# Softmax attention logits as three half-array products per head in two banks, in a written order

## The chip, the cores and the metric

The kernel runs on one core of one Trainium2 chip. A core has a matrix engine (TensorE, PE in the profile; its weight loads are listed apart, as PEld), a vector engine (VectorE, DVE), a scalar engine (ScalarE, ACT), a general one (GpSimd, POOL) and an engine that issues transfers (SyncE, SP). Each works through its own queue in order; semaphores tie the queues together. Matrix products are written to banks of PSUM, of 512 floats for each of 128 partitions, and read from there by DVE and ACT. The metric is the device time of one execution in microseconds (us). Before the change it is 2425.18 us, the median of 3 runs (2423.69 to 2426.76).

## What is computed

One decoder layer for 256 positions of width 2048 in float32: a SwiGLU network, a pair of token mixers beside each other (retention with 8 heads, and attention in a sliding window with 32 query heads over 8 key heads of dimension 64), and a second SwiGLU network. All projections of the mixers come from one product `h @ w_in`. The change is in the window attention:

```
def swa_with_sinks(q, k, v, sinks):
    ...
    kb, vb = band(k), band(v)
    logits = jnp.einsum('bnqhgd,bnkhd->bnhgqk', qb, kb).astype(jnp.float32) * (d ** -0.5)
    ...
    logits = jnp.where(valid[None, :, None, None], logits, NEG_INF)
    ...
    probs = jax.nn.softmax(jnp.concatenate([logits, sink], axis=-1), axis=-1)[..., :-1]
    out = jnp.einsum('bnhgqk,bnkhd->bnqhgd', probs.astype(v.dtype), vb)
```

The 256 positions are two blocks of 128. A query sees the 128 keys that end with its own position, or fewer at the start.

## The kernel before

**The large products.** Everything is done as products of 128x128 weights against 512 columns. A weight matrix is loaded as float32 (`raw`), cast to a short form by ACT (`wh`, L356), and the remainder is made by DVE (`wl`, L357). The activations are split in the same way (`hh`, `hl`). One product is then three matmuls, hi by hi, lo by hi and hi by lo (L348 to L350), which gather in two banks `pa`, one for each block `t` of 128 positions. One pass over 512 columns of a weight matrix is called a chunk here; its result needs two of the four banks of the pool `psa`. So the first product of a chunk can only start when the readers of the chunk before the last are done with their bank. Tiles called `raw`, `wh`, `wl` and `pa` come from pools, and a new one waits until the old one in its place has been read for the last time.

**The order of the chunks.** For `w_in` the chunks come as the queries of the window heads (four chunks), and later those of retention: its queries (RQ0, RQ1), its keys (RK0, RK1) and its values (RV0 and on). Retention's queries and keys are turned by a rotary embedding, which DVE does straight from the bank: L1326 (by the cosine) and L1332 (by the sine, twice), and L1337 and L1338 on what they gave. L227 is the sum on DVE that makes the layer's conditioning, of weights that stream in for it.

**The side work.** Between the matmuls of the chunks, generators in the list `side` run one step for each quarter of the depth of a chunk. For the window attention each pair of heads (16 pairs) is one generator, `window(pair)`. In its first step `window_weights` makes the logits, masks and exponentials; in the next one the weights of the pair before are turned by four transposes (L1253), masked (L1262, L1263), multiplied with the values (`window_values`, L1267 and L1275, of 64 columns, the two heads on the two column halves of the array) and copied out by ACT (L1278). Their banks `pd` come from the pool `psd` of two, taken by `side_bank()`.

**The logits.** Head dimension 64 takes half of the 128 partitions. The queries of each head are kept with the hi part on one half of the partitions and the lo part on the other; the keys (`keys`, `homes`, `other`) are there on both halves. A matmul over 128 partitions so adds hi and lo of the query at once, and two of them, with hi and lo of the key, make a logit: four products, lo by lo among them. For a pair there are four matmuls with 256 columns (block 1: both halves of its window) in one bank and four with 128 columns (block 0) in the other (L1201). DVE reads them by L1208 (times the masks), L1209 (add) and L1210 (scale and mask of block 0), L1216 takes the maximum.

**What sets the order.** A scheduler decides the order of the instructions on each engine, by a model of costs; nothing in the window's code is ordered by hand. Each engine then keeps that order.

**The query split.** For a chunk of queries and a block, four transposes (L1301) put the queries into a bank; then, for each of two halves, ACT casts (L1307) and DVE subtracts on 64 partitions.

Of the kernel before, what the change touches and what calls it, by code (L numbers as in the profile page):

```python
# [9 lines left out]
F32 = mybir.dt.float32  # L10
F32R = mybir.dt.float32r
AF = mybir.ActivationFunctionType
ALU = mybir.AluOpType
# [3 lines left out]
P = 128  # L17
S = 256
# [12 lines left out]
QH, KVH, HD = 32, 8, 64  # L31
# [46 lines left out]
def layer_kernel(  # L78
# [22 lines left out]
    nc = tc.nc  # L101
# [16 lines left out]
    def nm(s):  # L118
        uid[0] += 1
        return f"{s}_{uid[0]}"  # L120
# [4 lines left out]
    def bank():  # L125
        return psm.tile([P, CH], F32, tag="ps", name=nm("ps"))

    def side_bank():
        return psd.tile([P, CH], F32, tag="pd", name=nm("pd"))

    def t512():
        return tmp.tile([P, CH], F32, tag="t512", name=nm("t"))
# [7 lines left out]
    def small(n, tag):  # L140
        return two.tile([P, n], F32, tag=tag, name=nm(tag))
# [218 lines left out]
    def pair_tile():  # L360
        return asp.tile([P, 2, CH], F32, tag="a", name=nm("a"))
# [46 lines left out]
    def gemm(act, w, col0s, KT=KD, ready=None):  # L408
        banks = [[acc_bank() for _ in range(NT)] for _ in col0s]
        for kb in range(KT // KB):  # L410
            gemm_part(act, w, col0s, banks, kb, KT, ready if kb == 0 else None)
            step()
        return banks
# [454 lines left out]
    banks, moved = {}, set()  # L868
# [104 lines left out]
    with tc.manual_schedule(engines=ORDERED):  # L973
# [21 lines left out]
        for _ in range(3):  # L995
# [8 lines left out]
            out=s2, in_=ssq.rearrange("p (t i) -> p t i", t=NT), axis=AX.X, op=ALU.add  # L1004
        )
        nc.vector.tensor_scalar(
            out=v2, in0=s2, scalar1=1.0 / D, scalar2=EPS, op0=ALU.mult, op1=ALU.add
# [6 lines left out]
            out=q2, in0=q2, scalar1=-0.5, scalar2=1.5, op0=ALU.mult, op1=ALU.add  # L1014
# [85 lines left out]
    for g, ks in enumerate(groups):  # L1100
# [7 lines left out]
        for i, n in enumerate(order):  # L1108
            if i < first_i:
                continue  # L1110
            at = i - first_i
# [25 lines left out]
    def in_chunk(c0, ready=None):  # L1137
        return gemm(held, wi, [c0], ready=ready)[0]
# [10 lines left out]
    keys = one.tile([P, 2, KVH, S], F32R, tag="x", name="keys")  # L1149
    b = in_chunk(O_SV, ready)  # L1150
    for t in range(NT):
        for g in range(2):
# [8 lines left out]
            for j in range(4):  # L1161
                js = slice(j * P, (j + 1) * P)
                nc.tensor.transpose(ps[:, js], kd[:, js], ident)
            hi, lo = (
                keys[:, i, g * 4 : g * 4 + 4, t * P : (t + 1) * P] for i in range(2)
            )
            p4 = ps.rearrange("p (h s) -> p h s", h=4)
# [4 lines left out]
    for t in range(NT):  # L1172
# [4 lines left out]
    queries = [  # L1177
        v.rearrange("p (j a s) -> p j a s", j=4, a=2)
        for v in (homes[:, : KD * P], other, homes[:, : KD * P], homes[:, KD * P :])
    ]  # L1180
# [3 lines left out]
    pick, causal, own = masks[:, : 2 * P], masks[:, 2 * P : 3 * P], masks[:, 3 * P :]  # L1184

    def twice(v):
        return v[:, None, :].broadcast_to([P, 2, v.shape[1]])

    def window_weights(pair):


        kv = pair // 2
        both = pair_tile()
        lg, parts = both[:, :, :S], both[:, :, S:]
        banks = [side_bank(), side_bank()[:, :S]]
        of_t = [v.rearrange("p (i s) -> p i s", i=2) for v in banks][::-1]
        for i in range(2):
            qs = queries[pair // 4][:, pair % 4, i, :]
            for t in (1, 0):
                for n in range(2):  # L1200
                    nc.tensor.matmul(  # L1201
                        of_t[t][:, i, :],
                        qs[:, t * P : (t + 1) * P],
                        keys[:, n, kv, : (t + 1) * P],
                        start=n == 0,
                        stop=n == 1,
                    )
        nc.vector.tensor_mul(parts, of_t[1], twice(pick))  # L1208
        nc.vector.tensor_add(lg[:, :, :P], parts[:, :, :P], parts[:, :, P:])  # L1209
        nc.vector.scalar_tensor_tensor(  # L1210
            out=lg[:, :, P:], in0=of_t[0], scalar=HD**-0.5, in1=twice(causal),
            op0=ALU.mult, op1=ALU.add,
        )
        mx = small(4, "mx")
        m2 = mx.rearrange("p (i t) -> p i t", t=2)
        nc.vector.tensor_reduce(  # L1216
            out=m2, in_=lg.rearrange("p i (t s) -> p i t s", t=2), axis=AX.X, op=ALU.max
        )
        sb = sink_b[:, 2 * pair : 2 * pair + 2]
        nc.vector.tensor_tensor(  # L1220
            out=m2, in0=m2, in1=sb[:, :, None].broadcast_to([P, 2, 2]), op=ALU.max
        )
        ng = small(4, "ng")
        nc.vector.tensor_scalar(out=ng, in0=mx, scalar1=-1.0, scalar2=None, op0=ALU.mult)
        se = small(4, "se")
        nc.vector.tensor_tensor(
            out=se.rearrange("p (i t) -> p i t", t=2),
            in0=ng.rearrange("p (i t) -> p i t", t=2),
            in1=sb[:, :, None].broadcast_to([P, 2, 2]),
            op=ALU.add,  # L1230
        )
        nc.scalar.activation(se, se, AF.Exp)
        sm = small(4, "sm")
        for i in range(2):
            for z in (2 * i, 2 * i + 1):
                seg = lg[:, i, z % 2 * P : (z % 2 + 1) * P]
                nc.scalar.activation(
                    seg, seg, AF.Exp, bias=ng[:, z : z + 1], accum_out=sm[:, z : z + 1]
                )
        nc.vector.tensor_add(sm, sm, se)  # L1240
        nc.vector.reciprocal(sm, sm)
        l4 = lg.rearrange("p i (t s) -> p i t s", t=2)
        s4 = sm.rearrange("p (i t) -> p i t", t=2)[:, :, :, None]
        nc.vector.tensor_mul(l4, l4, s4.broadcast_to([P, 2, 2, P]))
        return lg
# [36 lines left out]
    def window(pair):  # L1282
        lg = window_weights(pair)
        yield
        if before:
            window_values(*before.pop())
        before.append((pair, lg))
        if pair == QH // 2 - 1:
            yield
            window_values(*before.pop())  # L1290
        yield

    for ci in range(4):
        b = in_chunk(O_SQ + ci * CH)
        for t in range(NT):
            u = t512()
            nc.any.tensor_copy(u, b[t])
            ps = bank()
            for j in range(4):
                js = slice(j * P, (j + 1) * P)  # L1300
                nc.tensor.transpose(ps[:, js], u[:, js], ident)  # L1301
            q4 = queries[ci]
            p4 = ps.rearrange("p (j s) -> p j s", j=4)
            for a in range(2):
                here, there = (slice(c * HD, (c + 1) * HD) for c in (a, 1 - a))
                hi = q4[here, :, a, t * P : (t + 1) * P]
                nc.scalar.copy(hi, p4[here])  # L1307
                nc.vector.tensor_sub(
                    q4[there, :, a, t * P : (t + 1) * P], p4[here], hi.bitcast(F32)
                )  # L1310
        side += [window(pair) for pair in range(ci * 4, ci * 4 + 4)]


# [1 line left out]
    for a, off in ((0, O_RQ), (1, O_RK)):  # L1315
        for ci in range(2):
            b = in_chunk(off + ci * CH)
            for t in range(NT):
                u = t512()
                v = t512()  # L1320
                p4 = b[t].rearrange("p (h a d) -> p h a d", h=4, a=2)
# [107 lines left out]
    for p in range(2):  # L1429
        sg = first if p == 0 else gates(p)  # L1430
        c0s = [(2 * p + i) * CH for i in range(2)]
        for g, a, w in ((1, a_swa, w_swa_branch), (0, a_ret, w_ret_branch)):
            banks = gemm(a, w[0], c0s)
# [109 lines left out]
```

## Time and profile before

The profiled execution took 2424.6 us; its span, from the first instruction's start to the last one's end, is 2422.8 us, so 1.8 us lie around it.

| what | value |
|---|---|
| median of 3 runs | 2425.18 us |
| profiled execution: time, span | 2424.6 us, 2422.8 us |
| mean granted TensorE clock | 0.995 |
| window attention's logits (L1201): first and last start | 853.3, 1082.9 us |
| logits matmuls (L1201) in the trace | 128, half of 256 columns and half of 128 |
| subtraction of weights (L357, DVE) | 784 times, 1205 ns each |
| cast of weights (L356, ACT) | 784 times, 1040 ns each |

In rows of a timeline the columns are the start in us, the duration in us, the engine, the line, the operation, the tiles written and read, and the shape; behind a time in square brackets stands the idle time before it and what ended it. Rows with "x4" stand for four instructions in a row, and their duration reaches from the first start to the last end. A matmul's duration is longer than its share of the stream, since matmuls overlap: the distance from start to start tells what one costs. In rows of lines, the columns are the engine, the line, the operation, the tiles, the count, the duration in nanoseconds (least, median, most), and the first and last start.

### The profile page before, as it was taken

How to read it: one execution, taken by the hardware profiler on the slowest of the kernel's cores; microseconds unless marked ns; L12 is line 12 of the kernel's file. 1: busy time of each engine (PE TensorE's matmuls, PEld its weight loads, DVE VectorE, ACT ScalarE, POOL GpSimd, SP SyncE). 2: the span in 40 equal slices, each digit the busy share in tenths (PEclk: the TensorE clock that was granted, in tenths of full speed). 3: DMA queues.
4: the chain of work that ended last, by engine and by line, in shares of the span. 5: the costliest groups of instructions: out<-in, count | busy, mean ns of one | idle time of the engine just before them, and what ended most of it. 6: DMA issues, size and time to landing. Idle time of an engine off the chain costs nothing.

```text
span 2422.8 us, 28701 instructions
## 1 busy us (share of the span) xinstructions
PE 2389.5 (99%) x10820; PEld 1965.7 (81%) x10820; DVE 1710.0 (71%) x2497; ACT 1184.8 (49%) x1604; POOL 8.3 (0%) x19
## 2 busy tenths in 40 slices
PE   7999999999999999999999999999999999999998
PEld 5887888888888888778888888888888888888886
DVE  7888787778977688886666776768565555545656
ACT  6644554444446455554444444456444444444544
POOL 0000000000000000000000000000000000000000
PEclk9999999999999999999999999999999999999999
DMA  9987668988876666656677777755666666665563
GB/s 362 336 293 287 224 259 330 341 314 322 319 280 230 231 238 213 239 207 227 243 261 255 249 260 274 265 191 191 211 242 224 226 226 234 235 224 190 185 200 122
DMA packets 244542, 603.32 MB, mean 249 GB/s; under 512 B 9809, under 2 KB 10193, under 8 KB 224817
## 3 DMA queue, kind: packets, MB, share of 16 engines
q1 hardware_dynamic: 242850, 591.61, 68.6%
q0 software_dynamic: 1552, 9.87, 1.1%
q8 instruction: 85, 1.39, 0.2%
q14 instruction: 55, 0.45, 0.1%
HBM read 597.22 MB, written 4.22 MB: 248 GB/s over the span
## 4 chain that ended last, share of the span: by engine, by line
PE 95%; DMA 2%; DVE 2%; issue 0%; ACT 0%; SPq 0%; DVEq 0%; ACTq 0%
PE pa L350 29%; PE pa L349 29%; PE pa L348 28%; PE pa L724 1%; DMA slot<-in_w_ada_dram 1%; PE pd L348 1%; PE pd L350 1%; PE pd L349 1%; PE ps L466 1%; PE pd L1201 1%; DVE wl L357 0%; PE pd L1267 0%; DMA x_sb<-in_x_dram 0%; PE pd L1253 0%; DVE slot L227 0%
## 5 line engine op out<-in xcount | busy, mean ns | idle before, releaser
L357 DVE TENSOR_TENSOR wl<-raw,wh 128x1024 fp32r<-128x1024 f32 (+1 forms) x784 | 941.0, 1205 | 586.5 <-ACT wh L356 584.8
L356 ACT CAST wh<-raw 128x1024 fp32r<-128x1024 f32 (+1 forms) x784 | 815.2, 1040 | 997.2 <-PE pa L349 941.7
L348 PE MATMUL pa<-wh,hh 128*128 128x512 f32 x2014 | 788.2, 391 | 3.9 <-DVE t L1332 3.0
L349 PE MATMUL pa<-wh,hl 128*128 128x512 f32 x2014 | 787.0, 391 | 0.0
L350 PE MATMUL pa<-wl,hh 128*128 128x512 f32 x2014 | 725.9, 392 | 0.0
L348 PEld LDWEIGHTS pa<-wh,hh 128*128 128x128 f32 x2014 | 378.7, 188 | 82.9 <-ACT wh L356 5.1
L349 PEld LDWEIGHTS pa<-wh,hl 128*128 128x128 f32 x2014 | 378.7, 188 | 77.1
L350 PEld LDWEIGHTS pa<-wl,hh 128*128 128x128 f32 x2014 | 376.6, 188 | 76.4
L349 PE MATMUL pa<-wh,a 128*128 128x512 f32 x992 | 384.1, 389 | 0.7 <-DVE a L389 0.7
L348 PE MATMUL pa<-wh,a 128*128 128x512 f32 x992 | 367.2, 390 | 1.1 <-ACT wh L356 0.9
L350 PE MATMUL pa<-wl,a 128*128 128x512 f32 x992 | 367.0, 390 | 0.6 <-DVE wl L357 0.6
L348 PEld LDWEIGHTS pa<-wh,a 128*128 128x128 f32 x992 | 185.8, 188 | 41.3 <-ACT wh L356 1.8
L349 PEld LDWEIGHTS pa<-wh,a 128*128 128x128 f32 x992 | 186.2, 188 | 40.0 <-DVE a L389 1.5
L350 PEld LDWEIGHTS pa<-wl,a 128*128 128x128 f32 x992 | 186.1, 188 | 39.9 <-DVE wl L357 1.6
L227 DVE CUSTOM_DVE_ANT_0 slot<-slot,cact 128x1024 f32<-128x1024 f32 (+1 forms) x126 | 182.3, 1474 | 18.6 <-DMA slot<-in_w_ada_dram 18.4
L227 DVE CUSTOM_DVE_ANT_0 raw<-raw,cact 128x512 f32<-128x512 f32 (+1 forms) x260 | 166.7, 694 | 27.0 <-DMA raw<-in_w_ada_dram 25.8
L389 DVE TENSOR_TENSOR a<-slot,a 128x512 fp32r<-128x512 f32 x124 | 84.6, 684 | 4.8 <-ACT a L388 4.8
L388 ACT CAST a<-slot 128x512 fp32r<-128x512 f32 x124 | 76.4, 618 | 5.3 <-PE pa L350 5.2
L348 PE MATMUL pd<-wh,hh 128*128 128x512 f32 x144 | 56.7, 395 | 0.7 <-DVE slot L947 0.7
L349 PE MATMUL pd<-wh,hl 128*128 128x512 f32 x144 | 56.7, 394 | 0.0
L467 ACT COPY slot<-ps 128x512 f32<-128x512 f32 x68 | 37.6, 585 | 31.8 <-PE ps L466 31.7
L350 PE MATMUL pd<-wl,hh 128*128 128x512 f32 x144 | 51.9, 397 | 0.0
(240 smaller groups left out, 1372.2 us busy)
## 6 DMA issues: line engine op xcount, KB each, us to landing
raw<-in_w_ffn_gu_dram SPq DMA_DIRECT2D x148, 1024.0 KB, 4.9
raw<-in_w_in_dram SPq DMA_DIRECT2D x104, 1024.0 KB, 5.0
raw<-in_w_ffn_down_dram SPq DMA_DIRECT2D x88, 1024.0 KB, 5.2
slot<-in_w_ada_dram SPq DMA_DIRECT2D x78, 1024.0 KB, 7.4
raw<-in_w_ada_dram SPq DMA_DIRECT2D x64, 1024.0 KB, 4.9
raw<-in_w_ffn_gu_dram SPq DMA_DIRECT2D x25, 768.0 KB, 7.5
raw<-in_w_swa_branch_dram SPq DMA_DIRECT2D x16, 1024.0 KB, 5.4
raw<-in_w_ret_branch_dram SPq DMA_DIRECT2D x16, 1024.0 KB, 5.3
```

The lines of the kernel that those rows point to most:

```text
L227: nc.vector.tensor_tensor_reduce(out=w[:, at], in0=w[:, at], in1=cact[:, at], scale=1.0, scalar=0.0, op0=ALU.mult, op1=ALU.add, accum_out= ...
L348: nc.tensor.matmul(ps, ah[:, j, ts], wh[:, j, :], start=first, stop=False)
L349: nc.tensor.matmul(ps, al[:, j, ts], wh[:, j, :], start=False, stop=False)
L350: nc.tensor.matmul(ps, ah[:, j, ts], wl[:, j, :], start=False, stop=last)
L356: nc.scalar.copy(hi, src)
L357: nc.vector.tensor_sub(lo, src, hi.bitcast(F32))
L388: nc.scalar.copy(hi, v)
L389: nc.vector.tensor_sub(lo, v, hi.bitcast(F32))
L466: nc.tensor.transpose(ps[:, j * P : (j + 1) * P], src_of(j), ident)
L467: nc.any.tensor_copy(dest, ps[:, : n * P])
L724: nc.tensor.matmul(banks[t], a[:, j, t * P : (t + 1) * P], wt[:, j, :], start=(kb, hs[0], n) == (0, 0, 0), stop=(kb, hs[-1], n) == (KD // ...
L1201: nc.tensor.matmul(of_t[t][:, i, :], qs[:, t * P : (t + 1) * P], keys[:, n, kv, : (t + 1) * P], start=n == 0, stop=n == 1,)
```

## The change

The logits of a pair are made of three products per head, hi by hi, lo by hi and hi by lo, over the 64 partitions on which the head lies; the product of lo by lo is left out. For this the split of the queries puts hi and lo of a head on the same partitions, as two tiles. Each head of a pair has a bank of its own, both blocks of a head beside each other in it, and the order in which TensorE takes the twelve matmuls is written out: block 1, then block 0, the terms in turn, and within a term head 1 and then head 0. The reads become one multiplication of 256 and one scaling of 128 columns per head and one add for both. The query split becomes one cast and one subtraction on all 128 partitions.

```diff
-        banks = [side_bank(), side_bank()[:, :S]]
-        of_t = [v.rearrange("p (i s) -> p i s", i=2) for v in banks][::-1]
+        banks = [side_bank() for _ in range(2)]
+        terms = ((0, 0), (1, 0), (0, 1))
+        with tc.manual_schedule(engines={mybir.EngineType.PE}):
+            for t, at in ((1, slice(0, S)), (0, slice(S, S + P))):
+                for n, (of_q, of_k) in enumerate(terms):
+                    for i in (1, 0):
+                        here = slice(i * HD, (i + 1) * HD)
+                        nc.tensor.matmul(
+                            banks[i][:, at],
+                            queries[pair // 4][here, pair % 4, of_q, t * P : (t + 1) * P],
+                            keys[here, of_k, kv, : (t + 1) * P],
+                            start=n == 0,
+                            stop=n == len(terms) - 1,
+                        )
         for i in range(2):
-            qs = queries[pair // 4][:, pair % 4, i, :]
-            for t in (1, 0):
-                for n in range(2):
-                    nc.tensor.matmul(
-                        of_t[t][:, i, :],
-                        qs[:, t * P : (t + 1) * P],
-                        keys[:, n, kv, : (t + 1) * P],
-                        start=n == 0,
-                        stop=n == 1,
-                    )
-        nc.vector.tensor_mul(parts, of_t[1], twice(pick))
+            nc.vector.tensor_mul(parts[:, i, :], banks[i][:, :S], pick)
+            nc.vector.scalar_tensor_tensor(
+                out=lg[:, i, P:], in0=banks[i][:, S : S + P], scalar=HD**-0.5, in1=causal,
+                op0=ALU.mult, op1=ALU.add,
+            )
         nc.vector.tensor_add(lg[:, :, :P], parts[:, :, :P], parts[:, :, P:])
-        nc.vector.scalar_tensor_tensor(
-            out=lg[:, :, P:], in0=of_t[0], scalar=HD**-0.5, in1=twice(causal),
-            op0=ALU.mult, op1=ALU.add,
-        )
...
-            for a in range(2):
-                here, there = (slice(c * HD, (c + 1) * HD) for c in (a, 1 - a))
-                hi = q4[here, :, a, t * P : (t + 1) * P]
-                nc.scalar.copy(hi, p4[here])
-                nc.vector.tensor_sub(
-                    q4[there, :, a, t * P : (t + 1) * P], p4[here], hi.bitcast(F32)
-                )
+            hi, lo = (q4[:, :, a, t * P : (t + 1) * P] for a in range(2))
+            nc.scalar.copy(hi, p4)
+            nc.vector.tensor_sub(lo, p4, hi.bitcast(F32))
```

The lines move by one to three: the matmuls of the logits are L1202 now, their reads L1210, L1211 and L1215, the maximum L1218, the transposes L1255, the masks of the turned weights L1264 and L1265, the products with the values L1269 and L1277, ACT's copy L1280, and the rotary products L1324 and L1330.

On TensorE, at the end of chunk RV0 and the start of RV1, stood this before (`pa_8268` and `pa_8269` are the two banks of RV0, `pa_8509` the first of RV1, `pd` the banks of the side work):

```order
4322 L348 MATMUL pa_8268<-wh_8473,hh_4047 128x512
4323 L349 MATMUL pa_8268<-wh_8473,hl_4048 128x512
4324 L1201 MATMUL pd_8158<-keys,homes_6263 128x128 x4
4325 L350 MATMUL pa_8268<-wl_8474,hh_4047 128x512
4326 L1253 MATMUL pd_8224<-small_c,a_8039 128x128 x4
4327 L348 MATMUL pa_8269<-wh_8473,hh_4047 128x512
...
4334 L349 MATMUL pa_8269<-wh_8473,hl_4048 128x512
4335 L350 MATMUL pa_8269<-wl_8474,hh_4047 128x512
4336 L348 MATMUL pa_8509<-wh_8513,hh_4047 128x512
```

The matmuls of 256 columns of the same pair stand 20 rows above. Now the same place reads so (`pa_8378` and `pa_8379` are the banks of RV0, `pa_8637` the first of RV1, `pd_8258` and `pd_8259` the banks of the two heads):

```order
4455 L1277 MATMUL pd_8216<-t_8212,slot_6259 64x128 x2
4456 L1202 MATMUL pd_8259<-keys,homes_6263 128x256
4457 L350 MATMUL pa_8378<-wl_8602,hh_4047 128x512
...
4460 L350 MATMUL pa_8379<-wl_8602,hh_4047 128x512
4461 L1202 MATMUL pd_8258<-keys,homes_6263 128x256
4462 L1202 MATMUL pd_8259<-keys,homes_6263 128x256
...
4470 L1202 MATMUL pd_8259<-keys,homes_6263 128x128
4471 L1202 MATMUL pd_8258<-keys,homes_6263 128x128
4472 L1255 MATMUL pd_8334<-small_c,a_8131 128x128 x4
4473 L348 MATMUL pa_8637<-wh_8641,hh_4047 128x512
```

The first matmul of head 1 stands alone behind the products with the values, and the other eleven, both widths, have moved from some rows ahead of the chunk's end to its very end, with the transposes behind them.

On VectorE, at the same place, stood before (`a` is the pair's tile of logits, `t` are the tiles of the turned weights and of the rotary embedding, which reads the banks `pa` of RK1):

```order
1222 L357 TENSOR_TENSOR wl_8514<-raw_8511,wh_8513 128x1024
1223 L1210 SCALAR_TENSOR_TENSOR a_8156<-pd_8158,slot_6259 128x2x128
1224 L357 TENSOR_TENSOR wl_8533<-raw_8511,wh_8532 128x1024
1225 L1216 TENSOR_REDUCE mx_8170<-a_8156 128x4
1226 L1262 TENSOR_TENSOR t_8230<-pd_8224,slot_6259 128x256
1227 L1326 TENSOR_TENSOR t_8240<-pa_8000,small_c 128x512
1228 L1332 TENSOR_TENSOR t_8241<-pa_8000,small_c 128x4x64 x2
```

The sums L227 that belong to this part of the program stand ahead of these rows, at 1206 to 1214. Now:

```order
1239 L357 TENSOR_TENSOR wl_8695<-raw_8692,wh_8694 128x1024
1240 L1210 TENSOR_TENSOR a_8257<-pd_8259,slot_6259 128x256
1241 L1211 SCALAR_TENSOR_TENSOR a_8257<-pd_8259,slot_6259 128x128
1242 L1210 TENSOR_TENSOR a_8257<-pd_8258,slot_6259 128x256
1243 L1211 SCALAR_TENSOR_TENSOR a_8257<-pd_8258,slot_6259 128x128
1244 L227 ISA raw_8806,sums_6302<-raw_8806,cact 128x512
...
1252 L1215 TENSOR_TENSOR a_8257<-a_8257 128x2x128
1253 L1264 TENSOR_TENSOR t_8340<-pd_8334,slot_6259 128x256
1254 L1324 TENSOR_TENSOR t_8350<-pa_8092,small_c 128x512
1255 L1330 TENSOR_TENSOR t_8351<-pa_8092,small_c 128x4x64 x2
```

The four reads of the logits, and four sums L227 behind them, have moved in between the weights' subtraction and the rotary products.

## The prediction

> **What bounds the kernel now.** I read the page first, its busy shares and its chain of waits, then the windows around the attention stage, the lines of the logits, and last the timelines of TensorE (PE) and VectorE (DVE) at the places that the change moves.
>
> ```profile
> PE 2389.5 (99%) x10820; PEld 1965.7 (81%) x10820; DVE 1710.0 (71%) x2497; ACT 1184.8 (49%) x1604; POOL 8.3 (0%) x19
> PE 95%; DMA 2%; DVE 2%; issue 0%; ACT 0%; SPq 0%; DVEq 0%; ACTq 0%
> L348 PE MATMUL pa<-wh,hh 128*128 128x512 f32 x2014 | 788.2, 391 | 3.9 <-DVE t L1332 3.0
> ```
>
> PE is busy 99% of the span and carries 95% of the chain: whatever lengthens PE's own stream, or makes it stand, is paid in full, and work taken from another engine pays nothing unless PE waits for it. The only waits of PE inside the projection stage are the 3.0 us of the third row, for the rotary products of DVE.
>
> ```profile
> core 0: us, PE busy (x) PEld busy (x) DVE busy (x) ACT busy (x) POOL busy (x), PEclk, DMA share, GB/s
> 850.00:1090.00 240.00, 236.97 (x1206) 192.30 (x1205) 204.23 (x425) 128.50 (x276) 1.58 (x3) 0.99 0.63 223
> 1025.00:1030.00 5.00, 3.11 (x9) 2.37 (x9) 4.84 (x13) 2.82 (x11) 0.00 (x0) 0.75 0.57 202
> ```
>
> In the stage that holds all the logits DVE is busy 204 of 240 us, 85%, and in the stretch where PE waits, 4.84 of 5 us. It has little to give there, and its order counts.
>
> **Part 1: the matmuls of the logits.** Before, a pair costs four matmuls of 256 columns and four of 128, on the whole array:
>
> ```profile
> 860.46 0.39 PE L349 MATMUL pa<-wh,hl 128*128 128x512 f32 x1
> 860.68 0.63 PE L1201 MATMUL pd<-keys,homes 128*128 128x256 f32 x4
> 861.15 0.39 PE L350 MATMUL pa<-wl,hh 128*128 128x512 f32 x1
> ...
> 958.57 0.56 PE L1201 MATMUL pd<-keys,other 128*128 128x128 f32 x4
> 958.97 0.44 PE L350 MATMUL pa<-wl,hh 128*128 128x512 f32 x1
> 959.25 0.40 PE L348 MATMUL pa<-wh,hh 128*128 128x512 f32 x1
> ```
>
> From start to start the four of 256 take 0.47 us. The four of 128 take 0.40 and the product behind them 0.28 in place of 0.23: 0.45. So 0.92 us a pair; a narrow one is no faster than a wide one, about 0.11, so weights, not columns, set its pitch. After, there are twelve on half the rows, six of each width, the two heads in turn. The trace has no half-row matmul. The nearest row is a half-column one, two heads beside each other:
>
> ```profile
> 895.62 0.39 PE L348 MATMUL pa<-wh,hh 128*128 128x512 f32 x1
> 895.94 0.65 PE L1267 MATMUL pd<-t,slot 128*64 128x256 f32 x4
> 896.42 0.39 PE L1275 MATMUL pd<-t,slot 128*64 128x128 f32 x4
> 896.74 0.74 PE L1201 MATMUL pd<-keys,homes 128*128 128x256 f32 x4
> 897.32 0.39 PE L349 MATMUL pa<-wh,hl 128*128 128x512 f32 x1
> ```
>
> Four half tiles of 256 take 0.48 us, as long as four whole ones; the four of 128 take 0.32, of which some 0.1 is the change back. So they stream one after the other, 0.11 for 256 columns and 0.055 for 128, with weights hidden. By that row the twelve take 6 x 0.11 + 6 x 0.055 = 0.97 us, 0.05 more than before. The bounds: heads side by side, 6 x 0.11 = 0.68 (0.24 less); nothing hidden, 12 x 0.11 = 1.33 (0.41 more). I take 0.97, the value of the nearest row; over 16 pairs 0.8 us, with ends at -3.9 and +6.6.
>
> The same rows price a change of the array's shape. From 895.62 to 897.32 are 1.70 us; one product (0.23), the half tiles (4 x 0.11 + 4 x 0.055 = 0.66) and four whole ones (0.47) make 1.36. The rest, 0.35, is two changes, 0.17 each: the first half tile comes 0.32 behind a product where the pitch is 0.23. The Trainium skill, "TensorEngine Tiling (Array Packing)", section Key Properties, says that changing the tiling mode drains TensorE, and that tiles run independently; the first speaks against this change, the second for it. By the first with the rows' price it is the sum below, by the second alone the lower end, -3.9.
>
> In the new order one lone logits matmul stands behind the half-column episode, and the other eleven follow some products later, since the other head's bank waits for ScalarE (ACT) to copy the previous pair's output. That adds, for about 15 of 16 pairs, three changes (0.5 us) and a lone unhidden matmul (0.1): about 9.2 us. **Part 1: +10 us.**
>
> **Part 2: what stands at the ends of the chunks.** Before, the narrow logits stand some 5 us ahead of the end of a chunk, and DVE reads them in that time. At the start of a chunk PE needs a bank that the rotary products of the chunk before the last must have read:
>
> ```profile
> 1022.30 0.56 PE L1201 MATMUL pd<-keys,homes 128*128 128x128 f32 x4
> ...
> 1024.12 0.60 PE L1253 MATMUL pd<-small_c,a 128*128 128x128 f32 x4
> 1024.47 0.47 PE L349 MATMUL pa<-wh,hl 128*128 128x512 f32 x1
> 1024.79 0.39 PE L350 MATMUL pa<-wl,hh 128*128 128x512 f32 x1
> 1027.06 0.47 PE L348 MATMUL pa<-wh,hh 128*128 128x512 f32 x1 [1.89 <-DVE t L1332]
> ...
> 1027.63 0.63 PE L350 MATMUL pa<-wl,hh 128*128 128x512 f32 x1
> 1028.06 0.63 PE L348 MATMUL pa<-wh,hh 128*128 128x512 f32 x1
> ...
> 1030.62 0.56 PE L348 MATMUL pa<-wh,hh 128*128 128x512 f32 x1
> ...
> 1057.53 0.47 PE L348 MATMUL pa<-wh,hh 128*128 128x512 f32 x1 [1.14 <-DVE t L1332]
> ...
> 1058.07 0.40 PE L350 MATMUL pa<-wl,hh 128*128 128x512 f32 x1
> 1058.30 0.40 PE L348 MATMUL pa<-wh,hh 128*128 128x512 f32 x1
> ```
> ```profile
> 1022.45 1.22 DVE L357 TENSOR_TENSOR wl<-raw,wh 128x1024 fp32r<-128x1024 f32 x1 [1.13 <-ACT wh L356]
> 1023.59 0.42 DVE L1210 SCALAR_TENSOR_TENSOR a<-pd,slot 128x256 f32<-128x256 f32 x1
> ...
> 1025.16 0.42 DVE L1262 TENSOR_TENSOR t<-pd,slot 128x256 f32<-128x256 f32 x1 [0.23 <-ACT t L1261]
> 1025.50 0.16 DVE L1224 TENSOR_SCALAR ng<-mx 128x4 f32<-128x4 f32 x1
> 1025.57 0.68 DVE L1326 TENSOR_TENSOR t<-pa,small_c 128x512 f32<-128x512 f32 x1
> 1026.17 0.74 DVE L1332 TENSOR_TENSOR t<-pa,small_c 128x256 f32<-128x256 f32 x2
> ```
>
> This stall of 1.89 us comes with a DVE that reached the logits 1.2 us ahead of the chunk's end. In the new order the run of eleven is the last work of a chunk at RK0, RK1, RV0 and RV1, and the rotary products are queued behind its four reads. Let T0 be the start of the chunk's last product. The weights' subtraction L357 stands ahead of the reads and waits for a cast that can start when that chunk's last products let go of its tile:
>
> ```profile
> 1021.36 1.05 ACT L356 CAST wh<-raw 128x1024 fp32r<-128x1024 f32 x1 [1.64 <-PE pa L349]
> 1077.43 0.69 DVE L227 CUSTOM_DVE_ANT_0 raw<-raw,cact 128x512 f32<-128x512 f32 x1
> ...
> 1079.27 0.69 DVE L1208 TENSOR_TENSOR a<-pd,slot 128x512 f32<-128x512 f32 x1
> L1359 DVE TENSOR_TENSOR t<-pd,dec x8: 278/280/281, 1104.5 to 1169.1; 128x128 f32<-128x128 f32 x8
> ```
>
> The last product of the tile's first half starts at T0 - 0.23 and takes 0.39, the cast 1.05, so the cast ends at about T0 + 1.2, and L357 holds DVE 1.14 (1022.45 to 1023.59), so the reads start at T0 + 2.4. At RV1: two multiplications of 256 (0.34 each from start to start, as 1025.16 to 1025.50) and two of 128 (0.28 long, some 0.22 apart) make 1.1; four conditioning sums L227, now queued between, 2.45 (1077.43 to 1079.27 for three); the add and the mask of the turned weights 0.34 each; the rotary products 0.60 and 0.74; and 0.15 until PE starts (1026.91 to 1027.06). That gives T0 + 8.1. Without the wait PE would be there at T0 + 1.75 (the run, a change back, four transposes, 0.35 in these rows). The stall is 6.4 us.
>
> RK1 has the same queue: 6.4. RV0 has a maximum over the logits (0.60) instead of the sums: 4.6. RK0 the same, with a later run: 4.0. At RQ1 the transposes of the weights wait for the reads' bank: 1.9; at RV2 for ACT's copies: 0.7. Together 24 us. Below, nothing, if DVE gets there earlier than I reckon; above, some 7 us more, if those casts wait longer.
>
> After before's stall the products came 0.43 apart from 1027.63 to 1030.62 where 0.23 is usual, with a granted clock of 0.75 in that window: 7 x 0.2 = 1.4 us; after the stall of 1.14 they came 0.23 apart. I add 1.4 for each of the four long stalls, 5.6 us. The Trainium skill, "TensorE: Matmul & The Clock Gate", Part 1, puts the return to half clock at an idle window of about 3.4 us, free running; by 3.4 us at half clock each long stall would lose 1.7 us, an estimate from that page, 6.8 in place of 5.6. Here a stall of 1.9 us was already enough.
>
> **Part 3: DVE and ACT.** The query split goes from 16 casts and 16 subtractions on half the partitions to 8 of each on all, and the reads of the logits become smaller and more. Both lie beside PE's products (99% busy), so I cost them at nothing; if that cover went, the four halved instructions a chunk would be worth a microsecond or two. No DMA is moved in number.
>
> **The sum**, against the profiled execution: its span is 2422.8 us and its time 2424.6, 0.6 below the median of the runs shown. 2424.6 + 10 (part 1) + 24 (stalls) + 5.6 (clock) - 4.4 (before's stalls of 1.89 and 1.14 and the clock after the first) = 2459.8; I say 2460. With part 1 at its ends it is 2455 and 2466; with stalls less by the 1.14 of L357, five times, 2454.
>
> **The rivals.** First, the ends of the chunks are covered: DVE gets to the rotary products as early as before, because weights are ready ahead or the four reads are short. Then part 1 alone remains, 2424.6 + 10 = 2435. DVE's 85% speaks against it, its quick short reads for it. Second, the other side, by one mechanism: the shapes change for nothing and half-row tiles of two heads run side by side, weights and all, so PE gives back 0.24 a pair, 3.9 us, and the logits are done so early that the stalls of before go too: 2424.6 - 3.9 - 4.4 = 2416. It decides at 0.24 / 3 = 0.08 us per change of shape; the half-column rows cost 0.17, so I give it little. Third, the change does less than it says: the gain of the pairs pays for the changes and the ends cost a little, 2425. Fourth, a PE that stands 6 us stays at the low clock longer, or its weights come late too: above 2472.
>
> **How the numbers follow.** The forecast, with its ends 2446 to 2472, has 0.58; covered ends (2435, 2430 to 2446) 0.16; the fourth rival 0.07; together slower by over 0.2% (4.85 us, about what a measurement of this kernel can tell from no change) 0.81. No change 0.09, faster 0.10. The range reaches from 2423 to 2472: it leaves out the faster rival, the fourth, and a little of the third.
>
> **What would show it.** Right: waits of PE for DVE's rotary products of 4 to 6 us each at the starts of four chunks, a granted clock near 0.75 behind them, a lead of 0.3 us ahead of each run of half-row matmuls, and a run of eleven in about 0.9 us. Wrong: no such waits (the first rival), pairs starting in 0.11 us for two heads without a lead (the second), or waits of PE for something not named here. The forecast falls if DVE takes the four reads well ahead of T0 + 2.4, or if L357 ahead of them isn't late.

## The result, and the profile after

The changed kernel takes 2463.73 us (median of 5 runs, 2460.82 to 2466.0), against 2425.18 us before: 1.0158 times as long, with a 95% interval of 1.0146 to 1.0169. That is 38.5 us more, where 2460 us was forecast. The profiled execution of after has a span of 2461.9 us, 39.1 us above the one of before, and nearly all of it lies in the attention stage: the first logits matmul starts at 854.0 us (853.3 before), and the last matmul with the values (L1269; L1267 before) at 1141.3 us (1102.7 before).

The page of after, its busy times, the engines' shares of the chain, and the group of the first products:

```profile
PE 2407.3 (98%) x10884; PEld 1971.2 (80%) x10884; DVE 1707.1 (69%) x2520; ACT 1179.7 (48%) x1597; POOL 8.2 (0%) x19
PE 95%; DVE 2%; DMA 1%; ACT 1%; issue 0%; SPq 0%; DVEq 0%; ACTq 0%
L348 PE MATMUL pa<-wh,hh 128*128 128x512 f32 x2014 | 793.3, 394 | 14.9 <-DVE t L1330 13.3
```

PE is busy 17.8 us longer (2407.3 against 2389.5; the row counts a matmul's time at a low clock as busy) and DVE and ACT are busy a little less, but the idle time ahead of the first products has grown from 3.9 to 14.9 us. The waits of PE in the stage, after (who waited, for whom, us in total, times, the longest):

```profile
PE pa L348 <- DVE t L1330: 13.3, 4, 4.4
PE pd L1255 <- DVE a L1211: 8.2, 5, 1.9
PE ps L1303 <- ACT t L1299: 0.9, 1, 0.9
PE pa L348 <- ACT slot L1394: 0.7, 1, 0.7
PE pd L1202 <- ACT slot L1280: 0.2, 1, 0.2
```

Together 23.3 us, where before had 3.0. The two large rows are the two halves of one queue: the transposes wait for DVE's last read of the logits, and then the next chunk's first product waits for the rotary products behind those reads. At the start of RV1, the place that the forecast worked out, PE's timeline of after reads:

```profile
1084.76 0.40 PE L350 MATMUL pa<-wl,hh 128*128 128x512 f32 x1
1085.08 0.90 PE L1202 MATMUL pd<-keys,homes 64*128 64x256 f32 x11
1087.89 0.66 PE L1255 MATMUL pd<-small_c,a 128*128 128x128 f32 x4 [1.91 <-DVE a L1211]
1092.80 0.80 PE L348 MATMUL pa<-wh,hh 128*128 128x512 f32 x1 [4.25 <-DVE t L1330]
1093.39 0.63 PE L349 MATMUL pa<-wh,hl 128*128 128x512 f32 x1
```

And DVE's at the same time:

```profile
1086.08 1.23 DVE L357 TENSOR_TENSOR wl<-raw,wh 128x1024 fp32r<-128x1024 f32 x1 [2.80 <-ACT wh L356]
1087.22 0.42 DVE L1210 TENSOR_TENSOR a<-pd,slot 128x256 f32<-128x256 f32 x1
...
1088.08 0.28 DVE L1211 SCALAR_TENSOR_TENSOR a<-pd,slot 128x128 f32<-128x128 f32 x1
1088.28 0.69 DVE L227 CUSTOM_DVE_ANT_0 raw<-raw,cact 128x512 f32<-128x512 f32 x1
...
1090.72 0.42 DVE L1215 TENSOR_TENSOR a<-a 128x256 f32<-128x256 f32 x1
1091.06 0.42 DVE L1264 TENSOR_TENSOR t<-pd,slot 128x256 f32<-128x256 f32 x1
1091.39 0.69 DVE L1324 TENSOR_TENSOR t<-pa,small_c 128x512 f32<-128x512 f32 x1
1091.99 0.75 DVE L1330 TENSOR_TENSOR t<-pa,small_c 128x256 f32<-128x256 f32 x2
```

T0 is 1084.76. DVE idles 2.80 us until ACT's cast is done, starts the subtraction at T0 + 1.32 and the reads at T0 + 2.46 (forecast 2.4); PE starts the next chunk at T0 + 8.04 (forecast 8.1). The windows show the granted clock (the third number from the end): it falls to 0.50 while PE still waits, at about 1090.4, and is back 6.8 us later.

```profile
1087.00:1090.40 3.40, 0.66 (x4) 0.42 (x4) 3.40 (x12) 0.37 (x1) 0.00 (x0) 1.00 0.12 48
1090.40:1093.80 3.40, 1.00 (x2) 0.83 (x3) 3.40 (x10) 0.00 (x0) 0.00 (x0) 0.50 0.50 146
1093.80:1097.20 3.40, 3.40 (x9) 2.64 (x8) 2.98 (x13) 1.12 (x6) 0.00 (x0) 0.50 0.44 167
1097.20:1100.60 3.40, 3.40 (x23) 2.42 (x22) 1.03 (x3) 0.99 (x6) 0.00 (x0) 1.00 0.00 0
```

### The profile page after: what moved, and what is told of

Its sections match the earlier page's. It is cut to its first block, busy times and chain, and to the rows that moved or that the text cites. A ratio compares the mean times of both kernels' runs of the same rounds, so it can differ in the third digit from the quotient of the medians.

```text
span 2461.9 us, 28834 instructions
## 1 busy us (share of the span) xinstructions
PE 2407.3 (98%) x10884; PEld 1971.2 (80%) x10884; DVE 1707.1 (69%) x2520; ACT 1179.7 (48%) x1597; POOL 8.2 (0%) x19
## 4 chain that ended last, share of the span: by engine, by line
PE 95%; DVE 2%; DMA 1%; ACT 1%; issue 0%; SPq 0%; DVEq 0%; ACTq 0%
PE pa L348 29%; PE pa L349 28%; PE pa L350 28%; PE pa L724 1%; PE pd L348 1%; PE pd L350 1%; PE pd L349 1%; PE ps L466 1%; DMA slot<-in_w_ada_dram 1%; PE pd L1202 1%; DVE wl L357 1%; PE pd L1269 0%; ACT wh L356 0%; DMA x_sb<-in_x_dram 0%; PE pd L1255 0%
## 5 line engine op out<-in xcount | busy, mean ns | idle before, releaser
L357 DVE TENSOR_TENSOR wl<-raw,wh 128x1024 fp32r<-128x1024 f32 (+1 forms) x784 | 941.7, 1207 | 613.6 <-ACT wh L356 611.5
L348 PE MATMUL pa<-wh,hh 128*128 128x512 f32 x2014 | 793.3, 394 | 14.9 <-DVE t L1330 13.3
L227 DVE CUSTOM_DVE_ANT_0 slot<-slot,cact 128x1024 f32<-128x1024 f32 (+1 forms) x126 | 182.5, 1476 | 39.1 <-DMA slot<-in_w_ada_dram 38.9
L227 DVE CUSTOM_DVE_ANT_0 raw<-raw,cact 128x512 f32<-128x512 f32 (+1 forms) x260 | 166.7, 696 | 25.7 <-DMA raw<-in_w_ada_dram 24.4
L455 DVE TENSOR_TENSOR wl<-raw,wh 128x1024 fp32r<-128x1024 f32 x34 | 41.4, 1223 | 13.9 <-ACT wh L452 13.4
```

What stands on the lines that cost most here:

```text
L227: nc.vector.tensor_tensor_reduce(out=w[:, at], in0=w[:, at], in1=cact[:, at], scale=1.0, scalar=0.0, op0=ALU.mult, op1=ALU.add, accum_out= ...
L348: nc.tensor.matmul(ps, ah[:, j, ts], wh[:, j, :], start=first, stop=False)
L357: nc.vector.tensor_sub(lo, src, hi.bitcast(F32))
L455: nc.vector.tensor_sub(self.lo, self.src, self.hi.bitcast(F32))
```

## The experiments

The theory to be tested: **the place**. The time goes because the logits are made at the very end of a chunk, so that DVE comes late to the rotary products and PE waits, and runs at a low clock behind the wait. The rival: **the shapes**. Half-row matmuls, the changes between shapes and the third product cost the time, and the waits would only be where it shows.

### The place without the shapes

The kernel before, with its eight whole-array matmuls, but an order for TensorE in which the banks alternate.

```diff
-        for i in range(2):
-            qs = ...
-            for t in (1, 0):
-                for n in range(2):
-                    nc.tensor.matmul(
+        with tc.manual_schedule(engines={mybir.EngineType.PE}):
+            for i in range(2):
+                for n in range(2):
+                    for t in (0, 1):
+                        nc.tensor.matmul(
...
```

> The kernel before, with its own eight whole-array matmuls a pair, but their order on TensorE written out so that the two banks alternate: most of a pair's matmuls wait for the later bank and stand at the end of the chunk, as in the changed kernel. No half-row matmul is in it. Theory of the place (the time goes into waits at the starts of chunks, because the logits are made last in the chunk): waits of PE for DVE at RQ1, RK0, RK1, RV0 and RV1 of together 15 to 25 us, 2440 to 2452 us. Rival (the half-row shapes and their changes cost the time): 2425 us, as before.

It took 2454.54 us, 1.0124 times before (1.0109 to 1.0139): some 30 us are lost with no half-row matmul at all. Its PE timeline at a chunk's start:

```profile
1009.94 0.97 PE L1201 MATMUL pd<-keys,homes 128*128 128x256 f32 x7
1011.26 0.66 PE L1253 MATMUL pd<-small_c,a 128*128 128x128 f32 x4 [0.35 <-DVE a L1210]
1014.92 0.79 PE L348 MATMUL pa<-wh,hh 128*128 128x512 f32 x1 [3.00 <-DVE t L1332]
1015.51 0.63 PE L349 MATMUL pa<-wh,hl 128*128 128x512 f32 x1
1015.94 0.63 PE L350 MATMUL pa<-wl,hh 128*128 128x512 f32 x1
```

Seven logits matmuls stand at the end, then transposes, then 3.00 us of waiting for L1332, then products 0.43 us apart. Its waits add up to 18.0 us. The time is 2.5 us above the range expected. The two profiled spans differ by 28.9 us. Of these 15.0 are waits (18.0 less 3.0) and 10.0 the low clock, which stands behind six waits here (56 products lie over 0.38 us apart, against 10 before). The order written for this test, with wide and narrow matmuls in turn, costs little by itself: counted from start to start, the logits matmuls take 17.1 us against 15.4. The likeness to the change is not complete: 2.8 us of these waits are at query transposes (L1301), where the changed kernel does not wait for DVE.

### The shapes without the place

The changed kernel with head 1's six matmuls first and then head 0's. The runs of six stand where before's fours stood, away from the ends of the chunks, but no two heads are in turn.

```diff
-            for t, at in ((1, slice(0, S)), (0, slice(S, S + P))):
-                for n, (of_q, of_k) in enumerate(terms):
-                    for i in (1, 0):
-                        here = slice(i * HD, (i + 1) * HD)
+            for i in (1, 0):
+                here = slice(i * HD, (i + 1) * HD)
+                for t, at in ((1, slice(0, S)), (0, slice(S, S + P))):
+                    for n, (of_q, of_k) in enumerate(terms):
```

> The changed kernel with the written order turned: the six matmuls of head 1 first, then the six of head 0. Two runs of six a pair, which stand where the wide and the narrow ones stood before, so not at the end of a chunk; but no two heads are beside each other and there is one more change of shape a pair than in the changed kernel. Theory of the place: waits at the chunks' starts back to 0 to 5 us, some 0.9 us a pair of shapes and lost overlap over the kernel before, 2434 to 2446 us. Rival (shapes): no faster than the changed kernel, 2464 us or more.

2437.91 us, 1.0057 times before (1.0042 to 1.0071), and 26 us less than the changed kernel. Its only wait for DVE in the stage:

```profile
PE pa L348 <- DVE t L1330: 2.1, 1, 2.1
```

So a kernel with all the half-row matmuls, and with more runs of them than the change has, loses only 13 us. Where that goes is in its timeline:

```profile
1006.46 0.90 PE L1202 MATMUL pd<-keys,homes 64*128 64x256 f32 x6
1007.29 0.50 PE L350 MATMUL pa<-wl,hh 128*128 128x512 f32 x1
```

Six of one head take 0.83 us with the change back. Counted from start to start, all the logits matmuls of this run take 26.1 us, against 15.4 before: that is most of the 13 us.

### A third bank

The changed kernel, but head 0's bank comes from the pool of the transposes, so that a pair waits less for the pair before.

```diff
-        banks = [side_bank() for _ in range(2)]
+        banks = [bank(), side_bank()]
```

> The changed kernel with the bank of head 0 taken from the pool of the transposes, so that the logits of a pair wait less for the bank of the pair before. Runs of twelve or of one and eleven, which stand a dozen rows or more from a chunk's end at five of six chunks. Theory of the place: 2426 to 2438 us, waits for DVE's rotary products under 5 us in all. Rival (shapes): no less than 2455 us.

2425.40 us, 1.0003 times before (0.9993 to 1.0012), 0.6 us under the range expected: the whole loss is gone, with every half-row matmul still there. The runs moved away from most chunk ends, and one wait of 0.8 us is left:

```profile
PE pa L348 <- DVE t L1330: 0.8, 1, 0.8
```

Here the two heads write to banks of different names, so that the timeline, which puts like rows together, shows them apart:

```profile
1043.86 0.38 PE L1202 MATMUL pd<-keys,homes 64*128 64x256 f32 x1
1043.87 0.38 PE L1202 MATMUL ps<-keys,homes 64*128 64x256 f32 x1
1044.09 0.27 PE L1202 MATMUL pd<-keys,homes 64*128 64x256 f32 x1
1044.09 0.27 PE L1202 MATMUL ps<-keys,homes 64*128 64x256 f32 x1
...
1044.69 0.50 PE L349 MATMUL pa<-wh,hl 128*128 128x512 f32 x1
```

The two starts of a pair fall within 0.01 us: the heads run side by side. All twelve, with the change back, take 0.83 us (1043.86 to 1044.69), as long as six of one head above.

### The rotary products off the banks

The changed kernel, with ACT copying each bank of retention's queries and keys to memory and DVE reading the copy.

```diff
+                out_of = t512()
+                nc.scalar.copy(out_of, b[t])
-                p4 = b[t].rearrange("p (h a d) -> p h a d", h=4, a=2)
+                p4 = out_of.rearrange("p (h a d) -> p h a d", h=4, a=2)
...
-                    b[t].rearrange("p (g d) -> p g d", d=64),
+                    out_of.rearrange("p (g d) -> p g d", d=64),
```

> The changed kernel with ScalarE copying each bank of retention's queries and keys to memory first, and the rotary products reading the copy, so that the banks come free without DVE. Theory of the place: the 13.3 us of waits for the rotary products go, with the low clock behind them, and the 8.2 us of the transposes' waits for the reads of the logits stay: 2443 to 2452 us. Rival (shapes): 2464 us as the changed kernel.

2447.77 us, 1.0092 times before (1.0076 to 1.0109), 16 us less than the changed kernel. Its waits:

```profile
PE pd L1255 <- DVE a L1211: 7.5, 6, 1.9
PE pa L348 <- ACT t L1320: 3.8, 4, 1.0
PE ps L1303 <- ACT t L1299: 1.0, 1, 1.0
PE pd L1202 <- ACT slot L1280: 0.5, 3, 0.2
```

The 13.3 us for the rotary products have become 3.8 us for ACT's copies, and the transposes still wait for the reads of the logits. Of the two kinds of wait one was so removed without the other.

### The query split

The changed kernel with as many casts and subtractions as before, on 64 partitions each.

```diff
-            nc.scalar.copy(hi, p4)
-            nc.vector.tensor_sub(lo, p4, hi.bitcast(F32))
+            for a in range(2):
+                here = slice(a * HD, (a + 1) * HD)
+                nc.scalar.copy(hi[here], p4[here])
+                nc.vector.tensor_sub(lo[here], p4[here], hi[here].bitcast(F32))
```

> The changed kernel with the query split done as two casts and two subtractions on 64 partitions each, as many as before the change. By the forecast's third part these lie beside PE's products and cost nothing: 2461 to 2466 us, no different from the changed kernel. Rival (the smaller split pays and hides a larger loss): 2467 us or more.

2462.44 us (2460.78 to 2467.5), 1.0162 times before (1.0148 to 1.0176), against 2463.73 us and 1.0158: no difference. The smaller split is worth nothing here that can be measured, as it was costed.

### Other banks, and whether a faster kernel is in reach

Head 1's bank in place of head 0's from the other pool:

> As third_bank, with head 1's bank in place of head 0's from the pool of the transposes: half of the pairs have all twelve matmuls in one run, and the others one and eleven; two runs stand near a chunk's end. Theory of the place and the price of shapes: 2422 to 2430 us. Rival (shapes free, place not decisive): the same as third_bank within 2 us whatever the waits show.

2430.29 us, 1.0026 times before (1.0016 to 1.0036), 0.3 us above the range expected, and not the same as third_bank, which the rival expected. Its one wait is 3.5 us:

```profile
1056.82 0.39 PE L350 MATMUL pa<-wl,hh 128*128 128x512 f32 x1
1057.05 0.60 PE L1255 MATMUL pd<-small_c,a 128*128 128x128 f32 x4
1061.11 0.47 PE L348 MATMUL pa<-wh,hh 128*128 128x512 f32 x1 [3.46 <-DVE t L1330]
```
```profile
1058.14 1.23 DVE L357 TENSOR_TENSOR wl<-raw,wh 128x1024 fp32r<-128x1024 f32 x1 [1.48 <-ACT wh L356]
1059.29 0.42 DVE L1264 TENSOR_TENSOR t<-pd,slot 128x256 f32<-128x256 f32 x1
1059.62 0.68 DVE L1324 TENSOR_TENSOR t<-pa,small_c 128x512 f32<-128x512 f32 x1
```

No logits stand there: the last of that chunk start at 1048.6, 8 us ahead of its end. What stands ahead of the rotary products on DVE is the subtraction of weights, held up 1.48 us by ACT's cast, and the mask of the turned weights.

The turned weights' bank from that pool too, so that more pairs have all twelve in one run:

> As third_bank, and the turned weights take their bank from the pool of the transposes too, so that more pairs have their twelve half-row matmuls in one run. By the price of a change of shape (two runs a pair cost some 0.4 us more than one) and with no wait at a chunk's start: 2420 to 2426 us, a little under the kernel before. Rival (banks now short for the rotary transposes, new waits of PE at other chunks): over 2428 us.

2425.29 us, 1.0009 times before (1.0000 to 1.0018), with waits of 1.7 and 0.9 us: inside the range expected, but not under the kernel before, and no gain over the third bank that can be measured.

The kernel before, with ACT's copies for the rotary products:

> The kernel before, with ScalarE copying each bank of retention's queries and keys to memory and the rotary products reading the copy. The theory of the place says that PE's two waits for DVE (3.0 us) and the low clock behind one of them (1.4 us) go: 2419 to 2423 us. Rival: ACT's copy is queued as late as DVE's products were and PE waits for it: 2424 us or more.

2423.88 us, 1.0005 times before (0.9996 to 1.0014). Its PE waits 1.8 us for the copies in place of 3.0 us for DVE. That lies between the two ranges expected, and nearer to the rival's (2424 or more): no difference.

The third bank and the copies in one:

> third_bank and rotary_copy in one: the half-row logits away from the chunks' ends, and the banks of retention's queries and keys freed by ScalarE's copies. third_bank has 0.8 us of waits for DVE left, so there is at most 1 us to win: 2422 to 2426 us, no difference from the kernel before that can be measured. Rival (a hidden cost of place that the waits do not show): under 2419 us.

2423.37 us, 0.9996 times before (0.9987 to 1.0005). No wait of PE in the stage is left in its trace, and it is no faster than before by more than the measurement tells. So no version here beats the kernel before.

The kernel before with a third bank:

```diff
-        banks = [side_bank(), side_bank()[:, :S]]
+        banks = [bank(), side_bank()[:, :S]]
```

> The kernel before, with the wide logits' bank taken from the pool of the transposes. Whole-array matmuls, three banks. By the waits alone, before's 3.0 us for DVE and 1.4 us of low clock could go: 2420 to 2424 us. Rival (the third bank helps only the half-row kernel, since before's logits were early already, and takes banks from the rotary transposes): 2425 us or more.

2446.55 us, 1.0088 times before (1.0074 to 1.0101), at least 22 us slower than the theory of the place expected by the waits alone; the rival (2425 us or more) held, though it named no such size. PE's and DVE's timelines at one chunk's start:

```profile
1038.17 0.39 PE L350 MATMUL pa<-wl,hh 128*128 128x512 f32 x1
1038.40 0.60 PE L1253 MATMUL pd<-small_c,a 128*128 128x128 f32 x4
1042.93 0.76 PE L348 MATMUL pa<-wh,hh 128*128 128x512 f32 x1 [3.93 <-DVE t L1332]
```
```profile
1039.89 1.23 DVE L357 TENSOR_TENSOR wl<-raw,wh 128x1024 fp32r<-128x1024 f32 x1 [1.45 <-ACT wh L356]
...
1041.11 0.42 DVE L1262 TENSOR_TENSOR t<-pd,slot 128x256 f32<-128x256 f32 x1
1041.44 0.68 DVE L1326 TENSOR_TENSOR t<-pa,small_c 128x512 f32<-128x512 f32 x1
1042.04 0.74 DVE L1332 TENSOR_TENSOR t<-pa,small_c 128x256 f32<-128x256 f32 x2
```

No logits are near (the last start at 1030.7, 7 us ahead). The scheduler put the transposes of the weights last in the chunk and the weights' subtraction ahead of the rotary products; DVE idles 1.45 us for ACT's cast, and PE waits 3.93 us. So it is not the logits as such, here as in third_bank_other: what stood between the chunk's last product and the rotary products in DVE's queue was paid by PE. In the changed kernel at RV1, too, this subtraction, with its wait for the cast, kept DVE until T0 + 2.46, so a part of the waits there is its and not that of the logits' reads; no run divides the two. A third bank is no remedy in itself; it moved the order well in one kernel and badly in the other.

## Why the prediction was right

**The place, and the stalls.** The forecast gave waits by chunk; the idle times in PE's timeline of after, added up at each chunk, give:

| chunk | forecast, us | measured, us |
|---|---|---|
| RQ1 | 1.9 | 2.8 |
| RK0 | 4.0 | 3.3 |
| RK1 | 6.4 | 6.3 |
| RV0 | 4.6 | 4.1 |
| RV1 | 6.4 | 6.2 |
| RV2 | 0.7 | 0.7 |
| sum | 24 | 23.3 |

The mechanism is shown from two sides: whole-array matmuls in that place lose 30 us, and half-row matmuls out of it lose nothing (third bank) or 13 us, mostly for lost overlap (heads apart). Two things came otherwise. At RQ1 the query transposes wait another 0.95 us for ACT. And at RK0, RK1, RV0 and RV1 the transposes of the weights wait for the reads of the logits too, 0.6 to 1.9 us, which the forecast had at RQ1 alone; so the waits for the rotary products themselves are 2.51, 4.40, 2.18 and 4.25 us, and only two of the four are the 4 to 6 us that were to show it. The sums by chunk are not touched by this, as both parts lie on the same way to the next chunk's first product.

**The clock.** Forecast 5.6 us for four stalls, less before's 1.4. Counted from the starts in the traces between 850 and 1150 us, 41 products of after lie over 0.38 us apart, which is 8.7 us more than at 0.227 each, against 10 products and 1.9 us before: a net 6.8 us where 4.2 was forecast. RQ1's stalls brought the low clock as well, and I had left that one out; and the five stretches cost from 1.1 to 2.3 us, 1.7 in the mean, not 1.4. The page of the Trainium skill named in the forecast, "TensorE: Matmul & The Clock Gate", Part 1, with its 3.4 us at half clock, gave 1.7 us for each as an estimate. The trace agrees in the mean and not in each: at RV1 the granted clock is 0.50 for 6.8 us, from 1090.4 to 1097.2, of which the part in the wait costs nothing and the rest 2.2 us. What sets it off is less than the page's idle window of 3.4 us: waits with no other near of 1.89 us (before) and 2.07 us (heads_apart, at 1066.04) brought it, while 1.14 us (before), 1.27 us (before_third_bank) and 1.66 us (third_bank_turned) did not.

**The shapes.** Of the 39.1 us of the profiled executions, 20.3 are waits (23.3 less 3.0) and 6.8 the clock; 12.0 are left for part 1 and all else, against a forecast of 10. That the two are near is luck in part, since the terms of that 10 were wrong, in opposite directions. The step that failed is "By that row the twelve take ... 0.97 us": the half-column rows were a poor likeness. The forecast read them as streaming one after the other, but single records of that trace show them in pairs as well (starts at 895.943 and 895.949, then at 896.209 and 896.216); only, a pair of 256 columns holds the stream for 0.21 us there, and a pair of half-row ones for 0.11 (1044.09 to 1044.20 in third_bank). Half-row matmuls of two heads run side by side, and a run of twelve costs 0.83 us with the change back, some 0.65 without (an estimate from the starts): the lower end, 0.68, not the value taken. The twelve are so cheaper in themselves than the eight whole ones, by about a quarter of a us a pair. What eats it is the changes of shape. That a change costs is also what the Trainium skill, "TensorEngine Tiling (Array Packing)", Key Properties, has with its rule that changing the mode drains TensorE. In after a lone matmul and its surroundings look so:

```profile
1083.64 0.38 PE L1202 MATMUL pd<-keys,homes 64*128 64x256 f32 x1
1083.95 0.50 PE L350 MATMUL pa<-wl,hh 128*128 128x512 f32 x1
1084.29 0.40 PE L348 MATMUL pa<-wh,hh 128*128 128x512 f32 x1
1084.53 0.39 PE L349 MATMUL pa<-wh,hl 128*128 128x512 f32 x1
```

The lone one takes 0.31, and the product behind it 0.34 where the pitch is 0.23: 0.42 us. A run of eleven has 0.09 ahead of it (1084.76 to 1085.08), takes 0.83, and adds 0.11 behind: 1.03. Together that is 1.45 us a pair. Before's 0.92 is too low for the comparison: behind the half-column tiles, where 12 of its 16 wide runs stand, four wide ones take 0.58 (896.74 to 897.32), so a pair took 1.03. The difference is 0.42, or 6 us for 15 pairs. Counted from start to start over all pairs, the logits and the products beside them cost 6.8 us more than before, the four transposes of the weights 2.0 us (7.7 against 5.7) and the other transposes 1.6 us; some 1.6 us of the 12.0 are not assigned, and why the transposes take longer was not tested. In third_bank the same matmuls stand in fewer runs and the waits are 2.2 us shorter than before's; its time is that of before, so shapes there cost no more than a few us.

**The rivals.** "The ends of the chunks are covered" (2435) is refuted by the waits; the other versions, heads_apart (2437.91) and third_bank (2425.40), are kernels in which most of the ends were covered. The faster rival needed shapes that change for nothing; half of it held, the heads do run side by side, and the other half, a price under 0.08 us a change, didn't: entering alone costs 0.09 and leaving 0.11 to the product behind, beside the change itself. Even with no wait left (third_bank_rotary_copy) the kernel is not measurably faster than before.

**Not tried.** Whether DVE's reads put behind the rotary products, with all else as changed, would remove the waits; whether the weights' subtraction L357 put behind them would do it without any move of the logits; and the four sums L227, which stand in the queue at RK1 and RV1, where the waits are about 2 us longer than at RV0, were not moved away by themselves.

## What to carry to other kernels

When a change touches a small part of a stage that a scheduler orders, look first at what its order does at the points where one engine hands a buffer to another: here 27 of 39 us were waits and low clock that came with the new order, and one word, the pool of a bank, took the whole loss back in one kernel and brought some 22 us on in the other. A saving in matmuls of a quarter of a us a pair was eaten by the changes of shape in every version here, and least so where the tiles of one shape stood together. And measure from the last product before the hand-over: a list of what stands in the waiting engine's queue from there, with durations from the profile, gave each of six waits to within 1 us.

## What the runs showed of the hardware

Matmuls of 64 rows on the two halves of the array, alternating, with outputs in different banks, start at the same time (1044.09 and 1044.09, third_bank): twelve take 0.83 us with the change of shape, as long as six of one half. The half-column ones here took as long as whole ones, 0.48 us for four of 256 columns, though two of them also start together. A wait of PE of 1.89 us (before) or 2.07 us (heads_apart) in a busy stretch was enough for eight or nine products at a low clock, 1.6 and 1.7 us more; waits of up to 1.66 us with no other near were not. Shorter ones close together were enough too: in rotary_copy waits of 0.16, 0.62 and 0.95 us within 3.3 us, up to 1045.02, had six such products behind them, 1.4 us more. So a wait near 2 us cost nearly its own length again here.
